# Summing a norm's squares on TensorE, feature tile by feature tile, in place of elementwise adds on POOL

## The chip, the cores and the metric

The kernel runs on one core of one Trainium2 chip. The metric is the device time of one execution in microseconds (us). The engines are named as the profile names them: PE is TensorE's matmul stream and PEld its weight loads, DVE is VectorE, ACT is ScalarE, POOL is GpSimd, SP is SyncE, whose queue issues the DMAs.

## What is computed

The reference is a two-layer encoder for 512 tokens of 1024 features in float32. Only its frame matters here:

```python
def rms_norm(x, g):
    y = xf * lax.rsqrt(jnp.mean(xf * xf, axis=-1, keepdims=True) + EPS)
    return (y * g.astype(jnp.float32)).astype(x.dtype)
...
    for l in range(DEPTH):
        h = rms_norm(x, attn_norm[l])
        proj = h @ w_in[l]
        ...                                  # four kinds of attention, 16 heads
        x = x + mix @ w_o[l]
        h = rms_norm(x, ffn_norm[l])
        x = x + (jax.nn.silu(h @ w_gate[l]) * (h @ w_up[l])) @ w_down[l]
    return rms_norm(x, final_norm)
```

So there are four norms ahead of dense products (attention and feed-forward, in two layers), and a final one. Each needs, for every token, the sum of the squares of its 1024 features.

## The kernel before

The activations lie transposed: x is eight tiles of 128 features by 512 tokens, x(0) to x(7). The norm isn't applied to the input of the products. `norm_inputs` makes from each x(k) the gained input, split in a high and a low part (`h[:, 0]` on ACT, or on DVE for odd k in the first norm; `h[:, 1]` by the scalar_tensor_tensor of line 209 on DVE), and the products run on these. The factor 1/rms of each token is multiplied into the results later. PE so doesn't need the sum of squares for its products, only whoever evacuates them does.

The sum of squares has two steps. `square` squares x(k) on ACT; the first square goes into the tile `ssq`, each later one into one of two buffers `sq`, which POOL adds to `ssq` (line 196), 128x512 elements at a time. After the eighth, `rms_column` lets PE sum over the 128 partitions: for each of four chunks of 128 tokens one product with the chunk of `ssq` as weights and one column of ones as the moving operand (line 225), into the first four columns of the PSUM bank "sm". DVE and POOL make the factor of it (`col`, `rcol`).

The four norms are called a0 (attention, layer 0), f0 (feed-forward, layer 0), a1 and f1 here. What surrounds each: a0 stands at the program's start, and its first consumer is the value projection `v_b` (line 382; weights `whi_vba`, `wlo_vba`, then `whi_vbb`, `wlo_vbb`, split from raw weights by ACT and DVE). f0 and f1 stand between the output projection (`wo`, whose results are added to x by DVE or, through a copy `po`, by POOL, line 609) and the gate and up products (`gu`, lines 178 to 183). a1 stands between the down products of layer 0 (`dn`) and `v_b` of layer 1.

Instructions are issued in order on each engine. What order that is, a scheduler decides when the program is built: it simulates the engines and places on each the instruction that it thinks ready first, in the program's order where several are. In attention a list of rates (`RATES`) mixes projections into the heads' work beforehand. The weights lie in four buffers `raw`, filled by DMAs from SP's queue.

Of the kernel before, what the change touches and what calls it, by code (L numbers as in the profile page):

```python
# [11 lines left out]
F32 = mybir.dt.float32  # L12
F32R = mybir.dt.float32r
AF = mybir.ActivationFunctionType
# [4 lines left out]
P = 128  # L19
D = 1024  # L20
S = 512
NL = 2
KD = D // P
# [41 lines left out]
def tile_encoder(ctx, tc, xT, gains, lamv, w_in, w_kr, w_d, w_o0, w_o1, w_o2, w_gu, w_dn,  # L65
                 t5, na_in, na_ed, onehot, crow, rope, na_mask, na_emask, out):
    nc = tc.nc
    pool = lambda name, **k: ctx.enter_context(tc.tile_pool(name=name, bufs=1, **k))

    cst = pool("cst")  # L70
# [9 lines left out]
    def stat_bank(nm):  # L80
        return ps.tile([P, 512], F32, tag="sm", name=nm, bufs=1)


    def wide(nm, dt=F32):

        return cst.tile([P, 2, S], dt, tag="h", name=nm, bufs=12)

    def res_tiles(nm):

        made = {}  # L90

        def at(k):
            if k // 2 not in made:
                made[k // 2] = wide(f"x{nm}{k // 2}")
            return made[k // 2][:, k % 2, :]

        return at, lambda k: at(k) is not None and made[k // 2]
# [8 lines left out]
    x, _ = res_tiles("in")  # L106
# [13 lines left out]
    ones = cst.tile([P, P], F32, name="ones")  # L120
# [69 lines left out]
    def square(acc, xk, k, nm):  # L190
        if k == 0:
            nc.scalar.activation(acc, xk, AF.Square)
            return
        sq = cst.tile([P, S], F32, tag="sq", name=f"sq_{nm}{k}", bufs=2)
        nc.scalar.activation(sq, xk, AF.Square)
        nc.gpsimd.tensor_tensor(acc, acc, sq, op=ALU.add)

    def norm_inputs(x, gcol, nm, lag, dve=()):

        hs = []  # L200
        acc = cst.tile([P, S], F32, tag="ssq", name=f"ssq_{nm}", bufs=1)
        for k in range(KD):
            h = wide(f"h_{nm}{k}", F32R)
            g = gn[:, gcol + k : gcol + k + 1]
            if k in dve:
                nc.vector.tensor_scalar(h[:, 0, :], x(k), g, None, op0=ALU.mult)
            else:
                nc.scalar.activation(h[:, 0, :], x(k), AF.Copy, scale=g)
            nc.vector.scalar_tensor_tensor(h[:, 1, :], x(k), g, h[:, 0, :].bitcast(F32),  # L209
                                           op0=ALU.mult, op1=ALU.subtract)  # L210
            hs.append(h)
            if k < lag:
                continue
            square(acc, x(k - lag), k - lag, nm)
        for k in range(KD - lag, KD):
            square(acc, x(k), k, nm)
        return hs, acc

    def rms_column(sums, n, nm, chunks=(0, 4), bank=None, mark=False):

        pt = bank or stat_bank(f"ms_{nm}")
        o = slice(0, chunks[1] - chunks[0])
        for c in range(*chunks):
            for i, t in enumerate(sums):
                mm = nc.tensor.matmul(pt[:, c - chunks[0] : c - chunks[0] + 1], t[:, c * P : (c + 1) * P], ones[:, :1],  # L225
                                 start=i == 0, stop=i == len(sums) - 1)
        col = cst.tile([P, 4], F32, tag="col", name=f"col_{nm}", bufs=4)
        nc.vector.tensor_scalar(col[:, o], pt[:, o], 1.0 / n, EPS, op0=ALU.mult, op1=ALU.add)
        r = cst.tile([P, 4], F32, tag="rcol", name=f"rcol_{nm}", bufs=4)
        nc.gpsimd.tensor_tensor(r[:, o], col[:, o], mhalf[:, o], op=ALU.pow)  # L230
        return (r, mm) if mark else r

    def spread_rows(r, nm, n, dst):

        pt = stat_bank(f"rows_{nm}")
        if n > 1:
            rep = cst.tile([P, S], F32, tag="sq", name=f"rep_{nm}", bufs=2)
            rep = rep.rearrange("p (c h d) -> p c h d", c=4, h=n)  # L240
            nc.vector.tensor_copy(rep, r.rearrange("p (h c) -> p c h", h=n).unsqueeze(3).to_broadcast([P, 4, n, P // n]))
        for c in range(4):
            col = r[:, c : c + 1].to_broadcast([P, P]) if n == 1 else rep[:, c].rearrange("p h d -> p (h d)")
            nc.tensor.transpose(pt[:, c * P : (c + 1) * P], col, ident)
        nc.scalar.copy(dst, pt)

    def rms_rows(r, nm):

        bc = cst.tile([P, S], F32, tag="bc", name=f"bc_{nm}", bufs=3)
        spread_rows(r, nm, 1, bc)  # L250
        return bc


    hs, ssq = norm_inputs(x, G_ATT, "a0", LAG0, HDVE)
# [50 lines left out]
    def attention(l, xsrc, x, hs, ssq, pl):  # L305
        k8 = lambda w, c: tuple(t.rearrange("p (k c) -> p k c", c=c) for t in w)
        ALL = slice(0, P)
        g = {}
# [62 lines left out]
        def v_tokens(lhs, rhs, nk, col, nm):  # L371

            v = g[f"v{nm}"] = v_tile(nm)
            pts = [acc_bank(f"v_{nm}{l}{i}") for i in range(2)]
            for k0 in range(0, nk, 4):
                for c in range(4):
                    o = pts[c // 2][:, (c % 2) * 256 : (c % 2) * 256 + 256]
                    t = slice(c * P, (c + 1) * P)
                    for k in range(k0, min(nk, k0 + 4)):
                        whi, wlo = rhs(k)  # L380
                        for i, (a, b) in enumerate(((0, whi), (1, whi), (0, wlo))):
                            nc.tensor.matmul(o, lhs[k][:, a, t], b, start=c % 2 == 0 and k == 0 and i == 0,
                                             stop=c % 2 == 1 and k == nk - 1 and i == 2, skip_group_check=True)
                            yield 0.5
                    if k0 + 4 >= nk and c % 2:
                        for i in (c - 1, c):
                            v_split(v, i, pts[i // 2][:, (i % 2) * 256 : (i % 2) * 256 + 256], col()[:, i : i + 1])

        def in_values(i, nm):
            wa = k8(slab(w_in[l, i], SLAB, nc.gpsimd, f"v{nm}a{l}"), 256)  # L390
            wb = k8(slab(w_in[l, i + 1], SLAB, nc.gpsimd, f"v{nm}b{l}"), 256)

            def col():
                if "rc" not in g:
                    g["rc"] = rms_column([ssq], D, f"at{l}")
                return g["rc"]

            yield from v_tokens(hs, lambda k: tuple(t[:, k % 4, :] for t in (wa if k < 4 else wb)), KD, col, nm)
# [512 lines left out]
        for part, ms in enumerate(PARTS):  # L911
            n = 4 // len(ms)
# [33 lines left out]
        for m, p, hh in HEADS:  # L946
            nm = "abcd"[m]
# [53 lines left out]
    def ffn(l, x, xpair, hs, ssq, pl):  # L1001
        turn = [0]

        def bank(nm):
            tag = ("acc", "sc", "tp")[turn[0] // 2 % 3]
            turn[0] += 1
            return ps.tile([P, 512], F32, tag=tag, name=nm, bufs=2)

        r_bc = rms_rows(rms_column([ssq], D, f"ff{l}"), f"ff{l}")
        act = []  # L1010
        for m in range(KF):
            pts = []
            for j in range(2):
                w = slab(w_gu[l, m, j], SLAB, nc.vector, f"gu{m}{j}{l}")
                w = tuple(t.rearrange("p (k c) -> p k c", c=P) for t in w)
                pt = bank(f"gu{m}{j}{l}")
                dense(pt, w, hs, slice(0, P))
                pts.append(pt)
            t = lambda n: pl.tile([P, S], F32, tag=n, name=f"{n}{m}_{l}", bufs=2)
            g, u, th = t("g"), t("u"), t("th")  # L1020
            nc.vector.tensor_tensor(g, pts[0], r_bc, op=ALU.mult)
            nc.scalar.activation(th, g, AF.Tanh, scale=0.5)
            nc.vector.scalar_tensor_tensor(u, pts[1], 0.5, r_bc, op0=ALU.mult, op1=ALU.mult)  # L1023
            nc.vector.scalar_tensor_tensor(th, th, 1.0, g, op0=ALU.add, op1=ALU.mult)
            nc.gpsimd.tensor_tensor(u, u, th, op=ALU.mult)  # L1025
            a = pl.tile([P, 2, S], F32R, tag="act", name=f"act{m}_{l}", bufs=KF)
            split(a[:, 0, :], a[:, 1, :], u)
            act.append(a)
        for m in range(KD - (l + 1 == NL)):
            pt = bank(f"dn{m}{l}")  # L1030
            for i, k0 in enumerate(range(0, KF, 8)):
                n = min(8, KF - k0)
                w = slab(w_dn[l, m][:, k0 * P : (k0 + n) * P], n * P, nc.vector, f"dn{m}{i}{l}")
                w = tuple(t.rearrange("p (k c) -> p k c", c=P) for t in w)
                dense(pt, w, act[k0 : k0 + n], slice(0, P), first=k0 == 0, last=k0 + n == KF)
            nc.vector.tensor_tensor(x(m), x(m), pt, op=ALU.add)
            if l + 1 < NL:
                nc.sync.dma_start(xd[:, m, :], x(m))
        if l + 1 == NL:
            last_tile(l, x, xpair, act, pl, bank)  # L1040
# [55 lines left out]
    for l in range(NL):  # L1096
        if l:
            hs, ssq = norm_inputs(x, G_ATT + KD * l, f"a{l}", 0)
        x, xpair = res_tiles(l)
        with tc.tile_pool(name=f"att{l}", bufs=1) as pl:  # L1100
            attention(l, xd if l else xT, x, hs, ssq, pl)
        hs, ssq = norm_inputs(x, G_FFN + KD * l, f"f{l}", 0)
# [127 lines left out]
```

## Time and profile before

| | us |
|---|---|
| median of 3 runs | 1343.3 (1340.87 to 1346.17) |
| profiled execution, its own time | 1343.78 |
| its span | 1342.0 |
| PE busy | 1290.7 (96% of the span), 6306 matmuls |
| PEld busy | 1066.8 (79%) |
| DVE busy | 773.3 (58%) |
| ACT busy | 561.3 (42%) |
| POOL busy | 469.8 (35%), 388 instructions |

The profiled execution's time is 1.8 us above its span and 0.5 us above the median. PE is busy almost all the time, the others about half of it or less; where PE stands still, the trace names the instruction that it waited for. An instruction's duration as listed includes time that overlaps with the next one; how much a stream of them takes is read from the distance between their starts.

### The profile page before, as it was taken

The page shows a single profiled execution, that of the slowest core. Times are in us where ns is not written, and L with a number is a line of the kernel's source. Part 1 is how long each engine was busy: PE and PEld are TensorE (multiplying, and loading weights), DVE is VectorE, ACT ScalarE, POOL GpSimd, SP SyncE. Part 2 cuts the span into 40 slices and gives each one's busy share as a digit, 9 for nine tenths or more (in the row PEclk, how much of TensorE's full clock was granted, in tenths as well). Part 3 has the DMA queues.
Part 4 walks back from the last instruction along what each step waited for, and adds up shares of the span by engine and source line. Part 5 has one row for each costly group of instructions (what it writes and reads, how often), then busy time and mean ns, then how long its engine had stood idle before and what let it go on. Part 6 is the DMA issues. An engine that isn't in the chain of part 4 may idle for free. (4 is left out here: it accounts for less than half of the span.)

```text
span 1342.0 us, 17137 instructions
## 1 busy us (share of the span) xinstructions
PE 1290.7 (96%) x6306; PEld 1066.8 (79%) x6306; DVE 773.3 (58%) x1309; ACT 561.3 (42%) x965; POOL 469.8 (35%) x388
## 2 busy tenths in 40 slices
PE   5998999999999999999999999999899999999997
PEld 5887878877888888888888777788688888888886
DVE  7499889866444444333236899887754444443232
ACT  3356656744333333232225666666533333332230
POOL 5257656535111111100135578454621111110100
PEclk9999999999999999999999899999999999999998
DMA  4552432112222222333345324322132222223321
GB/s 155 162 159 91 138 109 79 63 63 86 96 95 97 95 95 92 93 119 107 120 128 161 116 83 129 97 74 69 63 101 95 98 94 95 97 87 93 98 87 63
DMA packets 50484, 135.63 MB, mean 101 GB/s; under 512 B 7848, under 2 KB 12712, under 8 KB 50400
## 3 DMA queue, kind: packets, MB, share of 16 engines
q1 hardware_dynamic: 50400, 134.54, 32.2%
q8 instruction: 50, 0.82, 0.3%
q14 instruction: 34, 0.28, 0.1%
HBM read 119.01 MB, written 4.23 MB: 92 GB/s over the span
## 5 line engine op out<-in xcount | busy, mean ns | idle before, releaser
L180 PE MATMUL gu<-h_f,whi_gu 128*128 128x512 f32 x704 | 278.0, 395 | 1.3 <-DVE h_f L209 1.3
L178 PE MATMUL gu<-h_f,whi_gu 128*128 128x512 f32 x704 | 277.7, 395 | 0.1
L1025 POOL TENSOR_TENSOR u<-u,th 128x512 f32<-128x512 f32 x44 | 93.4, 2123 | 378.7 <-DVE u L1023 362.4
L183 PE MATMUL gu<-h_f,wlo_gu 128*128 128x512 f32 x704 | 177.9, 395 | 0.0
L180 PEld LDWEIGHTS gu<-h_f,whi_gu 128*128 128x128 f32 x704 | 132.5, 188 | 34.2 <-DVE h_f L209 3.9
L178 PEld LDWEIGHTS gu<-h_f,whi_gu 128*128 128x128 f32 x704 | 132.6, 188 | 31.7 <-DVE x L609 1.0
L183 PEld LDWEIGHTS gu<-h_f,wlo_gu 128*128 128x128 f32 x704 | 132.6, 188 | 30.9
L135 ACT CAST whi_gu<-raw_gu 128x1024 fp32r<-128x1024 f32 x88 | 92.5, 1052 | 112.5 <-PE gu L180 108.6
L178 PE MATMUL dn<-act,whi_dn 128*128 128x512 f32 x330 | 128.4, 389 | 0.0
L180 PE MATMUL dn<-act,whi_dn 128*128 128x512 f32 x330 | 128.4, 389 | 0.0
L165 DVE TENSOR_TENSOR wlo_gu<-raw_gu,whi_gu 128x1024 fp32r<-128x1024 f32 x88 | 110.8, 1259 | 20.0 <-ACT whi_gu L135 18.3
L632 ACT ACTIVATE e<-e,mx 128x512 f32<-128x512 f32 (+1 forms) x128 | 85.5, 669 | 66.7 <-DVE mx L630 61.5
L165 DVE TENSOR_TENSOR wlo_dn<-raw_dn,whi_dn 128x1024 fp32r<-128x1024 f32 (+1 forms) x45 | 51.0, 1134 | 100.4 <-PE dn L183 60.9
L1023 DVE SCALAR_TENSOR_TENSOR u<-gu,bc_ff 128x512 f32<-128x512 f32 x44 | 30.4, 691 | 128.5 <-PE gu L183 128.5
L135 ACT CAST whi_dn<-raw_dn 128x1024 fp32r<-128x1024 f32 (+1 forms) x45 | 44.2, 981 | 128.3 <-PE dn L180 111.3
L135 ACT CAST act<-u 128x512 fp32r<-128x512 f32 x44 | 27.3, 620 | 157.3 <-POOL u L1025 157.3
L183 PE MATMUL dn<-act,wlo_dn 128*128 128x512 f32 x330 | 82.1, 389 | 0.0
L140 DVE TENSOR_TENSOR tl<-tp,th 128x512 fp32r<-128x512 f32 x112 | 74.3, 681 | 7.8 <-ACT th L135 7.0
L630 DVE CUSTOM_DVE_ANT_0 e<-sc,t 128x512 f32<-128x512 f32 x96 | 65.0, 683 | 22.2 <-PE sc L697 19.5
L140 DVE TENSOR_TENSOR act<-u,act 128x512 fp32r<-128x512 f32 x44 | 32.7, 742 | 73.9 <-ACT act L135 73.6
L178 PEld LDWEIGHTS dn<-act,whi_dn 128*128 128x128 f32 x330 | 62.0, 188 | 12.9
L180 PEld LDWEIGHTS dn<-act,whi_dn 128*128 128x128 f32 x330 | 61.9, 188 | 12.9
(417 smaller groups left out, 2734.2 us busy)
## 6 DMA issues: line engine op xcount, KB each, us to landing
raw_gu<-in_w_gu_dram SPq DMA_DIRECT2D x88, 512.0 KB, 3.2
raw_dn<-in_w_dn_dram SPq DMA_DIRECT2D x32, 512.0 KB, 3.6
raw_wo<-in_w_o_dram SPq DMA_DIRECT2D x16, 512.0 KB, 4.0
t<-tb SPq DMA_DIRECT2D x16, 448.0 KB, 4.5
raw_dn<-in_w_dn_dram SPq DMA_DIRECT2D x16, 384.0 KB, 3.1
sb<-kbn SPq DMA_DIRECT2D x64, 64.0 KB, 2.0
sb<-qbn SPq DMA_DIRECT2D x64, 64.0 KB, 2.0
xin<-in_xT_dram SPq DMA_DIRECT2D x8, 256.0 KB, 5.9
```

The costliest lines, as they stand in the source:

```text
L135: nc.scalar.copy(out, src)
L140: engine(tag, usual).tensor_tensor(out, src, hi.bitcast(F32), op=ALU.subtract)
L165: lo_eng.tensor_tensor(lo[:, c], raw[:, c], hi[:, c].bitcast(F32), op=ALU.subtract)
L178: nc.tensor.matmul(pt, whi[:, k, wcol], xs[k][:, 0, :], start=first and k == 0, stop=False)
L180: nc.tensor.matmul(pt, whi[:, k, wcol], xs[k][:, 1, :], start=False, stop=False)
L183: nc.tensor.matmul(pt, wlo[:, k, wcol], xs[k][:, 0, :], start=False, stop=last and k == nk - 1)
L630: nc.vector.tensor_tensor_reduce(out=e, in0=sc, in1=bias, scale=1.0, scalar=BIG, op0=ALU.add, op1=ALU.min, accum_out=mx)
L632: nc.scalar.activation(e, src, AF.Exp, bias=mx, scale=-1.0, accum_out=den)
L1023: nc.vector.scalar_tensor_tensor(u, pts[1], 0.5, r_bc, op0=ALU.mult, op1=ALU.mult)
L1025: nc.gpsimd.tensor_tensor(u, u, th, op=ALU.mult)
```

## The change

For the four norms of `norm_inputs`, PE sums over the feature tiles too. Each square goes into a buffer `sq`, and four one-column products per tile (one per chunk of tokens) add it to the four columns of one PSUM bank, which the norm holds from its first product to its last. The tile `ssq`, POOL's adds and the four products at the end are gone there; what followed them is now `root_column`. The final norm keeps `square` and `rms_column`.

```diff
+    def square_sum(acc, xk, k, nm):
+        sq = cst.tile([P, S], F32, tag="sq", name=f"sq_{nm}{k}", bufs=2)
+        nc.scalar.activation(sq, xk, AF.Square)
+        for c in range(4):
+            nc.tensor.matmul(acc[:, c : c + 1], sq[:, c * P : (c + 1) * P], ones[:, :1], start=k == 0 and c == 0,
+                             stop=k == KD - 1, skip_group_check=True)
+
     def norm_inputs(x, gcol, nm, lag, dve=()):
         hs = []
-        acc = cst.tile([P, S], F32, tag="ssq", name=f"ssq_{nm}", bufs=1)
+        acc = stat_bank(f"ms_{nm}")
...
-            square(acc, x(k - lag), k - lag, nm)
+            square_sum(acc, x(k - lag), k - lag, nm)
...
-                    g["rc"] = rms_column([ssq], D, f"at{l}")
+                    g["rc"] = root_column(ssq, D, f"at{l}")
...
-        r_bc = rms_rows(rms_column([ssq], D, f"ff{l}"), f"ff{l}")
+        r_bc = rms_rows(root_column(ssq, D, f"ff{l}"), f"ff{l}")
```

Where the products stand in PE's queue is seen in the order of the built programs. In f0 before, PE had the four products of the sum (x4: four alike) between the second pair of gate and up weights and the third:

```order
L183 MATMUL gu010_3546<-h_f06_3478,wlo_gu010_3543 128x512
L183 MATMUL gu010_3546<-h_f07_3484,wlo_gu010_3543 128x512
L225 MATMUL ms_ff0_3493<-ones_93,ssq_f0_3443 128x1 x4
L178 MATMUL gu100_3588<-h_f00_3444,whi_gu100_3584 128x512
L180 MATMUL gu100_3588<-h_f00_3444,whi_gu100_3584 128x512
```

Now, on PE in f0, the products of the first squares stand among the last output projections (tiles 3 and 4 of `wo` are `wo230` and `wo240`):

```order
L183 MATMUL wo230_3412<-mix00_0_3312,wlo_wo200_3382 128x512
L183 MATMUL wo230_3412<-mix01_0_3374,wlo_wo200_3382 128x512
L204 MATMUL ms_f0_3464<-ones_93,sq_f00_3468 128x1 x4
L204 MATMUL ms_f0_3464<-ones_93,sq_f01_3477 128x1 x4
L178 MATMUL wo240_3429<-mix00_0_3312,whi_wo240_3424 128x512
L180 MATMUL wo240_3429<-mix00_0_3312,whi_wo240_3424 128x512
```

Squares 2, 3 and 4 follow behind `wo` tiles 5, 6 and 7, and squares 5, 6 and 7 among the first two `gu` tiles: eight fours in place of one, two of them side by side. f1 is alike.

In a1, on PE, all eight fours stand behind the last `dn` product; the first two are side by side, the other six among the products of `v_b`:

```order
L183 MATMUL dn70_5766<-act21_0_5154,wlo_dn720_5830 128x512
L204 MATMUL ms_a1_5854<-ones_93,sq_a10_5858 128x1 x4
L204 MATMUL ms_a1_5854<-ones_93,sq_a11_5867 128x1 x4
L396 MATMUL v_b10_5944<-whi_vba1_5932,h_a10_5855 128x256 x2
L396 MATMUL v_b10_5944<-wlo_vba1_5933,h_a10_5855 128x256
L396 MATMUL v_b10_5944<-whi_vba1_5932,h_a11_5864 128x256 x2
```

In a0 the first two fours stand ahead of PE's first product of `v_b`, the other six in three pairs among the 96 products of `v_b`: behind the 14th, the 40th and the 57th. On ACT in a0 before, the squares were mixed with the split of the second half of the weights (`whi_vbb`):

```order
L195 ACTIVATE sq_a05_137<-xin2_80 128x512
L135 CAST whi_vbb0_185<-raw_vbb0_183 128x512
L195 ACTIVATE sq_a06_140<-xin3_83 128x512
L135 CAST whi_vbb0_185<-raw_vbb0_183 128x512
L195 ACTIVATE sq_a07_143<-xin3_83 128x512
```

Now, on ACT in a0, four squares stand behind both halves of it:

```order
L218 ACTIVATE h_a06_118<-xin3_83,gn_69 128x512
L135 CAST whi_vbb0_211<-raw_vbb0_209 128x512 x2
L202 ACTIVATE sq_a04_148<-xin2_80 128x512
L202 ACTIVATE sq_a05_154<-xin2_80 128x512
L285 ACTIVATE lexp0_183<-lsum0_177 128x2
L285 ACTIVATE lexp1_193<-lsum1_187 128x2
L202 ACTIVATE sq_a06_160<-xin3_83 128x512
```

Away from the norms, the scheduler has also mixed the heads' scores and the projections differently in the first half of layer 0's attention; in layer 1's attention no instruction stands elsewhere.

## Rows read from the trace of the kernel before

**Rows 1.** Busy time by stretch: length, PE, PEld, DVE, ACT, POOL, granted clock, DMA:
```profile
0.00:31.00 31.00, 17.33 (x108) 16.22 (x109) 21.48 (x39) 12.29 (x21) 14.77 (x16) 0.94 0.52 167
306.00:331.00 25.00, 24.29 (x108) 18.83 (x107) 15.63 (x15) 10.93 (x15) 11.76 (x8) 1.00 0.25 85
667.00:686.00 19.00, 19.00 (x132) 17.71 (x131) 3.55 (x6) 3.83 (x5) 7.63 (x6) 1.00 0.54 163
961.00:986.00 25.00, 24.33 (x109) 19.02 (x109) 15.04 (x14) 10.36 (x14) 11.76 (x8) 1.00 0.25 85
130.00:140.00 10.00, 9.64 (x35) 7.88 (x36) 7.17 (x18) 5.49 (x12) 5.23 (x5) 0.70 0.18 52
```

**Rows 2.** PE's waits, whole run: us in total, times, longest:
```profile
PE v_b L382 <- DVE wlo_vbb L165: 3.3, 1, 3.3
PE v_b L382 <- DVE h_a L209: 2.9, 3, 1.4
PE gu L180 <- DVE h_f L209: 1.3, 4, 0.5
PE wo L178 <- DVE x L609: 1.0, 2, 0.7
```

**Rows 3.** PE in f0 in order of time: start, us, instruction:
```profile
319.05 0.95 PE L225 MATMUL ms_ff<-ones,ssq_f 128*128 128x1 f32 x8
319.86 0.47 PE L178 MATMUL gu<-h_f,whi_gu 128*128 128x512 f32 x1
320.17 0.39 PE L180 MATMUL gu<-h_f,whi_gu 128*128 128x512 f32 x1
320.40 0.39 PE L178 MATMUL gu<-h_f,whi_gu 128*128 128x512 f32 x1
```

**Rows 4.** DVE in a0 in order of time (wait in brackets):
```profile
6.80 0.48 DVE L206 TENSOR_SCALAR h_a<-xin,gn 128x512 fp32r<-128x512 f32 x1
7.32 2.30 DVE L209 SCALAR_TENSOR_TENSOR h_a<-xin,gn,h_a 128x512 fp32r<-128x512 f32 x2
10.15 1.50 DVE L206 TENSOR_SCALAR h_a<-xin,gn 128x512 fp32r<-128x512 f32 x1
20.27 1.40 DVE L209 SCALAR_TENSOR_TENSOR h_a<-xin,gn,h_a 128x512 fp32r<-128x512 f32 x2
```

**Rows 5.** POOL in a0 in order of time:
```profile
9.87 9.43 POOL L196 TENSOR_TENSOR ssq_a<-ssq_a,sq_a 128x512 f32<-128x512 f32 x6 [1.46 <-ACT sq_a L195]
```

**Rows 6.** PE in a0 in order of time:
```profile
9.68 0.58 PE L382 MATMUL v_b<-whi_vba,h_a 128*128 128x256 f32 x1 [1.39 <-DVE h_a L209]
...
22.64 0.40 PE L382 MATMUL v_b<-whi_vbb,h_a 128*128 128x256 f32 x2
...
23.00 0.40 PE L382 MATMUL v_b<-whi_vbb,h_a 128*128 128x256 f32 x2
...
23.94 0.63 PE L382 MATMUL v_b<-whi_vbb,h_a 128*128 128x256 f32 x2
...
24.58 0.63 PE L382 MATMUL v_b<-whi_vbb,h_a 128*128 128x256 f32 x2
...
26.50 0.55 PE L382 MATMUL v_b<-whi_vbb,h_a 128*128 128x256 f32 x2
...
30.17 0.39 PE L178 MATMUL sc_ip_kb<-h_a,whi_kb 128*128 128x512 f32 x1
```

**Rows 7.** ACT in order of time, in a0 and f0:
```profile
14.52 0.62 ACT L135 CAST whi_vbb<-raw_vbb 128x512 fp32r<-128x512 f32 x1 [1.07 <-DMA raw_vbb<-in_w_in_dram]
...
297.91 0.61 ACT L195 ACTIVATE sq_f<-x 128x512 f32<-128x512 f32 x1
```

**Rows 8.** PE in order of time: ends of both attentions, layer 1's start, one wait:
```profile
130.36 1.11 PE L772 MATMUL tp<-ident,e 128*128 128x128 f32 x4 [3.63 <-DVE e L702]
...
306.31 0.50 PE L178 MATMUL gu<-h_f,whi_gu 128*128 128x512 f32 x1
...
686.73 0.39 PE L178 MATMUL sc_ip_kb<-h_a,whi_kb 128*128 128x512 f32 x1
...
960.74 0.50 PE L178 MATMUL gu<-h_f,whi_gu 128*128 128x512 f32 x1
```

More of the change, by code (lines that the diff above doesn't have):

```diff
@@ L213, in norm_inputs @@
                 continue
-            square(acc, x(k - lag), k - lag, nm)
+            square_sum(acc, x(k - lag), k - lag, nm)
         for k in range(KD - lag, KD):
-            square(acc, x(k), k, nm)
+            square_sum(acc, x(k), k, nm)
         return hs, acc
@@ L226, in rms_column, with root_column @@
                                  start=i == 0, stop=i == len(sums) - 1)
+        r = root_column(pt, n, nm, o)
+        return (r, mm) if mark else r
+    def root_column(pt, n, nm, o=slice(0, 4)):
         col = cst.tile([P, 4], F32, tag="col", name=f"col_{nm}", bufs=4)
@@ L230, in rms_column @@
         nc.gpsimd.tensor_tensor(r[:, o], col[:, o], mhalf[:, o], op=ALU.pow)
-        return (r, mm) if mark else r
+        return r
     def spread_rows(r, nm, n, dst):
```

## The prediction

> **What bounds the kernel now.** I read the busy time by stretch first, around each of the four norms. In f0 and f1 PE is busy 24.3 of 25.0 us at the full granted clock, in a1 19.00 of 19.00 us; in a0, the first 31 us, only 17.3 [rows 1]. So at three of the four places whatever is added to PE's queue lengthens the run, unless it fills one of the short gaps, and at the fourth there are gaps. Whose they are, the waits of PE say: in a0 3.3 us for the low part of the weights `wlo_vbb` and 2.9 us for the low parts of h, in f0 and f1 together 1.3 us for the low part of h and 1.0 us for an addition to x [rows 2]. All of these come from DVE.
>
> Next I looked at what slows DVE there. In a0 the same tensor_scalar of 128x512 took 0.48 us at 6.80 and 1.50 us at 10.15, and two of the scalar_tensor_tensor took 2.30 us at 7.32 and 1.40 us at 20.27 [rows 4]. The long ones lie beside POOL's adds: six of these fill 9.87 to 19.30 without a gap [rows 5]. When POOL has finished, DVE is fast. The adds that the change removes are thus not free, though no chain of waits ends at their sum: they slow the engine that PE waits for.
>
> **What the change adds on PE.** The trace has the very operation: four one-column products of a 128x128 float32 weight tile. Each stands there as two matmul rows, and the four as x8. They start at 319.05, the next matmul at 319.86: 0.81 us, or 0.10 per row and 0.20 per product. The matmul behind them takes 0.31 to the one after it, where its neighbours take 0.23 [rows 3]. So a group of four costs 0.81 + 0.08 = 0.89 us, two groups side by side 2 x 0.81 + 0.08 = 1.70.
>
> The Trainium skill ("TensorE: Matmul & The Clock Gate", section "Back-to-back issue gap") lists a matmul of 1 to 64 columns at about 60 cycles, an issue floor of some 25 ns. By that the 112 added products, at two rows each, would cost an estimated 5.6 us, and the run would end near 1340. The row of 0.81 us for eight speaks against it here: something other than the column limits them, and the price of the row is measured in the same stream, so I take the row.
>
> f0, f1 and a1 each get eight groups, two of them side by side, in place of one: 1.70 + 6 x 0.89 - 0.89 = 6.15 us more. In a0 two groups stand ahead of `v_b`, where PE is idle anyhow: it waits until 9.68 but for two products [rows 6], and the first two squares need one early tile of x each. Were that cover gone, they would cost 1.70. The other three pairs cost 3 x 1.70 - 0.89 = 4.21. The bounds of the price: none, if the loads of the weights hid behind neighbouring matmuls (the group of rows 3 stands between 128x512 products and hid none), and, where the clock is low, 0.20 x 0.64 / 0.36 = 0.36 per product (that ratio from a0, below), which for a0's 24 products is 3.8 us more.
>
> **What it gives back.** In a0: the wait for `wlo_vbb`, 3.3; the waits for h behind the first one, 2.9 - 1.39 = 1.5; the start, since the two operations at 7.32 can take 1.40 in place of 2.30, 0.9; and the slow clock behind the long wait: from 23.94 to 26.50 three products take 0.64 us, where from 22.64 to 23.00 they take 0.36 [rows 6], 4 x 0.28 = 1.1. Together 6.8. For all of it to come, nothing else may be late. `whi_vbb` is released by its DMA at 14.52 [rows 7]; two halves of 0.6 on ACT and two of about 0.6 on DVE put the last `wlo_vbb` at 16.5. PE needs it behind 48 products and two pairs of groups: 8.8 + 14 x 0.21 + 34 x 0.12 + 3.4 = 19.2, so that wait is gone. Squares 4 and 5 stand behind `whi_vbb` on ACT and end at 14.52 + 4 x 0.6 = 16.9; PE comes to their products at 8.8 + 14 x 0.21 + 26 x 0.12 + 1.7 = 16.6 and waits 0.3, and all of `v_b` behind them waits with it. a0 is then worth -6.8 + 4.2 + 0.3 = -2.3. If DVE is slow for another reason, nothing comes back: +4.2.
>
> In f0 and f1: the 1.3 and 1.0 us of waits [rows 2], since POOL's additions to x (`po`) no longer queue behind adds of squares and DVE isn't slowed. Do the products wait for their squares there? Each comes behind an output tile or several `gu` products, 1 to 2 us apart, while ACT needs 0.61 for a square [rows 7], and a square waits only for the products of the one two before it. The worst case is x(7), which runs over PE, a copy on ACT, POOL's add, ACT's gain and the square, about 3.5 us behind the last output tile; its products stand 22 `gu` products and three groups later, 22 x 0.23 + 3 x 0.89 = 7.7 us. So I count no wait. Nor in a1: squares 2 to 7 now come late on ACT, only when PE has read the ones before them, but PE has 10 to 25 `v_b` products of 0.12 between pairs.
>
> What is removed from POOL, 28 adds, shortens nothing else: in a1 it worked in the shade of the `dn` products. The factor 1/rms comes earlier than before, and nobody waits for it.
>
> **Layer 0's attention** is mixed differently. I can't cost that row by row. There are two mixes of the same work in the trace: from the first `sc_ip_kb` to the first `gu` layer 0 takes 306.31 - 30.17 = 276.1 us [rows 6, 8] and layer 1 960.74 - 686.73 = 274.0 [rows 8]. They differ by 2.1; I take 0 and twice that difference, 4.2, to both sides.
>
> **Sum**: 3 x 6.15 - 2.3 (f0, f1) - 2.3 (a0) = +13.9 on the profiled 1343.8, 1357.7. That run lies 0.5 above the median, so 1357 is what I forecast for the median, 1.0% slower.
>
> **Rivals.**
> - *The passes hide behind their neighbours* (not slower). Then only edges remain: 24 groups or pairs less the 4 of before, 20 x 0.08 = 1.6, against 6.8 + 2.3 given back: 1336. For it speaks that PE loads weights ahead in dense streams; against it rows 3, measured in just such a stream. It decides only below 0.08 us per product, where 112 x 0.08 meets the 9.1 given back. Chance 0.04.
> - *The new mix of layer 0's attention removes its worst place.* A transpose waits 3.63 us for `e` at 130.36 [rows 8], and the granted clock is 0.70 in the ten microseconds there [rows 1], some 3.0 us lost: 13.9 - 6.6 = 7.3, 1350.5. All other waits of that mix would have to stay as they are. Chance 0.08.
> - *The relief doesn't come*, because DVE's long operations have another cause than POOL. Then 6.8 + 2.3 stay: 1366. Against it: with POOL's adds beside it the one tensor_scalar took three times as long. Chance 0.07.
> - *Products wait for squares.* PE's queue is in order; if at each of the 24 places ACT were half a square late, 24 x 0.3 = 7 us, 1364. With only two buffers `sq` ACT in turn waits for PE. From a whole square late at each place it is 1372. Chance 0.09.
>
> What is left, 0.72, is the forecast with its bounds: 1350 to 1362 from the attention's 4.2, half a microsecond of rounding at each norm, and parts of the relief missing or more. The rivals below and above leave some 0.1 on either side, so the range is 1350 to 1364. A difference of 0.5%, 6.7 us, is about what a measurement of this kernel can tell from none. Slower by more: the 0.72, the two slow rivals and a small part of the second, less a tail that meets the bound: 0.85. Within 0.5%: 0.11, most of it the attention's. Faster: 0.04, the first rival.
>
> **What would show it.** In the profile after, 0.81 us from the first to the end of a group, 0.10 per row; PE with 224 more matmul rows; the stretch from the first `gu` of f0 on shifted; a1 from the last `dn` to `sc_ip_kb` longer by 6.1 us with no wait named; in a0 DVE's scalar_tensor_tensor near 0.7 us each throughout, no wait for `wlo_vbb`, and `sc_ip_kb` starting near 28 in place of 30.17; layer 1's attention as long as before. The prediction is wrong if a group costs much less than 0.8 us, if waits for `sq` appear on PE, or if layer 0's attention moves by more than 4 us.

## The result

| | before | after |
|---|---|---|
| median, us | 1342.1 (1340.87 to 1346.17, 4 runs) | 1356.62 (1355.81 to 1357.4, 4 runs) |
| profiled execution, its own time | 1343.78 | 1355.97 |
| its span | 1342.0 | 1354.2 |

The changed kernel takes 1.0103 times as long, 95% interval 1.0078 to 1.0127: 14.5 us in the medians, 12.2 in the spans of the two profiled executions. The execution before that was profiled lies 1.7 us above its median, the one after 0.65 below.

The profile page of the changed kernel has this row of busy time (busy us, share, instructions):

```profile
PE 1314.4 (97%) x6530; PEld 1097.1 (81%) x6530; DVE 756.1 (56%) x1309; ACT 560.6 (41%) x965; POOL 424.2 (31%) x360
```

PE has the 224 added matmul rows (6306 before) and is busy 24 us longer; POOL is busy 46 us less and DVE 17 us less, and the run is longer all the same.

To see where 12.2 us went I cut the span of each kernel at eight places on PE that every kernel has: the end of `v_b` in a0, the `wo` product that waits some 1.7 us for DVE's `mix` near the end of an attention, the first `dn` product, the instruction behind the last `dn` product, the end of `v_b` in a1, and the same again in layer 1. For before these are 30.17, 291.36, 554.61, 674.35, 686.73, 946.08, 1209.02 and the span's end, 1342.0. Lengths in us, by differences of start times:

| kernel | a0 | att. 0 | f0, gu | dn 0 | a1 | att. 1 | f1, gu | rest | span |
|---|---|---|---|---|---|---|---|---|---|
| before | 30.17 | 261.19 | 263.25 | 119.74 | 12.38 | 259.35 | 262.94 | 132.98 | 1342.0 |
| after | 30.90 | 260.50 | 266.50 | 119.74 | 18.53 | 258.45 | 266.24 | 133.34 | 1354.2 |
| difference | +0.73 | -0.69 | +3.25 | 0 | +6.15 | -0.90 | +3.30 | +0.36 | +12.2 |
| predicted | -2.3 | 0 | +5.0 | 0 | +6.15 | 0 | +5.0 | 0 | +13.9 |

So the sum was right within 1.7 us, while the terms of a0, f0 and f1 were not; their errors have opposite signs.

**a1 and f0.** PE of the changed kernel in order of time, a1 first, then f0 (start, us, instruction).

```profile
677.64 1.84 PE L204 MATMUL ms_a<-ones,sq_a 128*128 128x1 f32 x16
679.34 0.48 PE L396 MATMUL v_b<-whi_vba,h_a 128*128 128x256 f32 x2
...
681.44 0.95 PE L204 MATMUL ms_a<-ones,sq_a 128*128 128x1 f32 x8
682.25 0.36 PE L396 MATMUL v_b<-wlo_vba,h_a 128*128 128x256 f32 x1
...
696.17 0.39 PE L178 MATMUL sc_ip_kb<-h_a,whi_kb 128*128 128x512 f32 x1
```

```profile
303.92 0.94 PE L204 MATMUL ms_f<-ones,sq_f 128*128 128x1 f32 x8
304.73 0.48 PE L178 MATMUL wo<-mix,whi_wo 128*128 128x512 f32 x1
```

In a1 a group takes 0.81 (681.44 to 682.25), as in [rows 3], the two side by side 1.70 (677.64 to 679.34), and nothing waits. The same 0.81 stands in f0, again without a wait in brackets. Of the waits of PE, whole run (us in total, times, longest), these two are of operands near a norm:

```profile
PE ms_a L204 <- ACT sq_a L202: 5.0, 1, 5.0
...
PE wo L178 <- DVE x L621: 0.4, 2, 0.3
```

The 5.0 for `sq_a` are the program's beginning. The list has no wait for `h_f`, for an operand of `v_b` or for a later square any more, and that of `wo` for x fell from 1.0 to 0.4 [rows 2].

**a0.** First DVE, then PE of the changed kernel, then busy time by stretch (length, PE, PEld, DVE, ACT, POOL, granted clock, DMA) for a0 and a1.

```profile
10.19 1.41 DVE L219 SCALAR_TENSOR_TENSOR h_a<-xin,gn,h_a 128x512 fp32r<-128x512 f32 x2
...
16.29 0.68 DVE L165 TENSOR_TENSOR wlo_vbb<-raw_vbb,whi_vbb 128x512 fp32r<-128x512 f32 x1
```

```profile
11.58 3.41 PE L204 MATMUL ms_a<-ones,sq_a 128*128 128x1 f32 x16
14.85 0.56 PE L396 MATMUL v_b<-whi_vba,h_a 128*128 128x256 f32 x1
...
15.42 0.63 PE L396 MATMUL v_b<-whi_vba,h_a 128*128 128x256 f32 x2
...
16.06 0.63 PE L396 MATMUL v_b<-whi_vba,h_a 128*128 128x256 f32 x2
...
20.54 1.88 PE L204 MATMUL ms_a<-ones,sq_a 128*128 128x1 f32 x16
22.29 0.37 PE L396 MATMUL v_b<-whi_vba,h_a 128*128 128x256 f32 x1
...
30.90 1.02 PE L303 MATMUL t<-oh,tab 32*8 32x512 f32 x2
```

```profile
0.00:31.00 31.00, 25.98 (x161) 25.83 (x162) 13.90 (x40) 12.30 (x21) 4.17 (x9) 1.00 0.54 167
677.60:696.20 18.60, 18.60 (x162) 18.56 (x161) 4.40 (x7) 5.24 (x9) 3.48 (x3) 1.00 0.48 148
```

DVE is as fast as was hoped: two scalar_tensor_tensor take 1.41 at 10.19, where [rows 4] had 2.30 for two, and the last `wlo_vbb` starts at 16.29. PE is busy 25.98 of 31 us, before 17.33 [rows 1], and yet `v_b` ends 0.73 us later. The reason is the distance of PE's rows. From 8.45 to 20.54 the products of `v_b` are 0.21 us apart (15.42 to 16.06 for three), and the pair at 11.58 takes 3.27; from 20.54 on a pair takes 1.75 and the products are 0.12 apart (three from 22.61 to 22.96). The ratio is that of PE's two clock levels, 1.2 and 2.4 GHz. The column of the granted clock says 1.00 for the whole stretch, so that here the spacing has to be read. Before, PE was at the wide spacing from 9.68 to 12.2 and once more, behind its long wait, up to 26.5 [rows 6].

### The profile page after: what moved, and what is told of

It reads as the page before. It is cut to its first block, busy times and chain, and to the rows that moved or that the text cites. A ratio compares the mean times of both kernels' runs of the same rounds, so it can differ in the third digit from the quotient of the medians.

```text
span 1354.2 us, 17562 instructions
## 1 busy us (share of the span) xinstructions
PE 1314.4 (97%) x6530; PEld 1097.1 (81%) x6530; DVE 756.1 (56%) x1309; ACT 560.6 (41%) x965; POOL 424.2 (31%) x360
## 5 line engine op out<-in xcount | busy, mean ns | idle before, releaser
L165 DVE TENSOR_TENSOR wlo_gu<-raw_gu,whi_gu 128x1024 fp32r<-128x1024 f32 x88 | 107.2, 1219 | 13.7 <-PE gu L183 10.5
L178 PEld LDWEIGHTS dn<-act,whi_dn 128*128 128x128 f32 x330 | 61.9, 188 | 13.0
L183 PEld LDWEIGHTS dn<-act,wlo_dn 128*128 128x128 f32 x330 | 62.0, 188 | 12.8
```

What stands on the lines that cost most here:

```text
L165: lo_eng.tensor_tensor(lo[:, c], raw[:, c], hi[:, c].bitcast(F32), op=ALU.subtract)
L178: nc.tensor.matmul(pt, whi[:, k, wcol], xs[k][:, 0, :], start=first and k == 0, stop=False)
L183: nc.tensor.matmul(pt, wlo[:, k, wcol], xs[k][:, 0, :], start=False, stop=last and k == nk - 1)
```

## Experiments

All ratios are to the kernel before, with the 95% interval; a time without a ratio is one run. Of each edit the lines that matter are shown. The parts of each kernel, cut as above:

| kernel | a0 | att. 0 | f0, gu | a1 | att. 1 | f1, gu | span |
|---|---|---|---|---|---|---|---|
| e1_no_adds | 23.10 | 260.40 | 262.78 | 12.30 | 258.09 | 261.70 | 1331.4 |
| e2_idle_adds | 28.42 | 262.02 | 266.25 | 18.53 | 259.55 | 266.50 | 1354.0 |
| e3_a0_late | 33.74 | 261.63 | 267.11 | 18.55 | 260.47 | 266.24 | 1360.3 |
| e4_f32r | 26.20 | 259.79 | 263.53 | 14.84 | 258.08 | 262.76 | 1337.6 |
| e5_late_squares | 22.23 | 270.78 | 263.45 | 12.38 | 257.90 | 262.77 | 1342.2 |
| e6_a1_block | 30.91 | 262.80 | 265.31 | 22.65 | 258.70 | 266.52 | 1360.0 |
| e7_ones_weights | 23.59 | 263.43 | 263.20 | 13.17 | 259.96 | 264.45 | 1340.2 |
| e8_cols32 | 27.00 | 260.49 | 266.21 | 18.56 | 260.90 | 266.22 | 1352.5 |
| e9_ones_a0 | 24.34 | 263.27 | 264.17 | 12.17 | 258.04 | 263.27 | 1337.6 |
| e10_f32r_a0 | 24.88 | 259.88 | 264.47 | 12.17 | 260.65 | 263.85 | 1338.4 |

One thing must be known to read the columns of f0 and f1: the long stream of `gu` products, which no edit touches, doesn't run at one pace everywhere. From each row of eight `wlo_gu` to the next are 24 products; here of e1_no_adds in f0:

```profile
326.01 2.03 PE L183 MATMUL gu<-h_f,wlo_gu 128*128 128x512 f32 x8
331.62 2.03 PE L183 MATMUL gu<-h_f,wlo_gu 128*128 128x512 f32 x8
```

Such a round takes 5.60 us on average in e3_a0_late, e4_f32r, e7_ones_weights, e9_ones_a0, e10_f32r_a0 and in f0 of e1_no_adds, and 5.577 in all others, f1 of e1_no_adds included, at a granted clock of 1.00 in both. Over the 44 rounds of such a part it makes 1.0 us. No trace here shows what decides it.

My theory ahead of the experiments: products cost 0.10 us a row wherever PE is the bound, and POOL's adds, by slowing DVE, were what made PE wait in a0, f0 and f1. The rival: POOL has no part in the waits; the products fill time that PE would have waited anyhow.

### The adds alone, taken away and put back

e1_no_adds, before with

```diff
-        nc.gpsimd.tensor_tensor(acc, acc, sq, op=ALU.add)
+        if nm == "fin":
+            nc.gpsimd.tensor_tensor(acc, acc, sq, op=ALU.add)
```

> The kernel before, with POOL's 28 adds of squares left out in the four norms (the sum then holds the first square alone); nothing is added on PE. If POOL's adds are what makes DVE late, PE loses its waits in a0 and its six late starts in f0 and in f1 (3.1 us each by the distance of the starts): v_b of a0 ends some 4 to 7 us earlier than at 30.17, f0 and f1 are 3 us shorter each, a1 as before; 1342 - 12 = about 1330. Rival 1, the products of the change filled the gaps and POOL's adds had no part in them: f0 and f1 as before, 1342 to 1336. Rival 2, DVE's long operations in a0 have another cause: a0 as before too, 1342.

Measured: 1333.44, ratio 0.9933 (0.9914 to 0.9953). PE in a0 (the next instruction behind `v_b`), and in f0:

```profile
23.10 1.02 PE L290 MATMUL t<-oh,tab 32*8 32x512 f32 x2
```

```profile
297.89 0.63 PE L183 MATMUL wo<-mix,wlo_wo 128*128 128x512 f32 x2
298.63 0.51 PE L178 MATMUL gu<-h_f,whi_gu 128*128 128x512 f32 x1
...
301.52 0.40 PE L178 MATMUL gu<-h_f,whi_gu 128*128 128x512 f32 x1
301.91 0.49 PE L180 MATMUL gu<-h_f,whi_gu 128*128 128x512 f32 x1
303.06 0.50 PE L178 MATMUL gu<-h_f,whi_gu 128*128 128x512 f32 x1 [0.65 <-ACT po L602]
```

a0 is relieved in full. `v_b` ends at 23.10, and one product `t` of 0.95 us, which comes behind it in the kernel before, lies inside: 30.17 - 23.10 + 0.95 = 8.0 us. 0.9 of it are the four products, which come ahead of `v_b` here; the other 7.1 are the relief that I put at 6.8. In f0 the gain is 0.47, in f1 1.24; without the slower `gu` rounds f0's would be 1.5. PE still starts late three times: 298.63 (0.74 behind two rows that need 0.46), 301.91 (0.39 in place of 0.23) and 303.06 (1.15 in place of 0.23), now for ACT's copy `po`. With the 0.10 that the instruction behind each late one loses where it stands at 0.33, that is 1.6 us, where the kernel before has 3.1 of the kind (below). So without POOL's adds about half of the lateness in f0 is gone. Some of that may be due to the four products of the sum and the four of `rows_ff`: they come earlier here, among the last `wo` tiles, and fill time as the products of the change do. The forecast of 3 us in each of f0 and f1 was more than twice what came.

e2_idle_adds, the changed kernel with

```diff
+        if k:
+            junk = cst.tile([P, S], F32, tag="ssq", name=f"jq_{nm}{k}", bufs=1)
+            nc.gpsimd.tensor_tensor(junk, sq, sq, op=ALU.add)
```

> The changed kernel, with POOL's 28 additions put back beside the products (each square is added to itself, into a tile that nobody reads). PE's order is that of the changed kernel. If POOL's adds slow DVE, DVE's scalar_tensor_tensor in a0 takes 1.1 to 1.8 us again; in f0 and f1 the late starts come back as far as the products haven't given DVE the time: 0 to 3 us each. My theory, that the relief comes from POOL, says 1357 to 1363. Rival, the products alone took the waits away by delaying PE: 1356.6 within 1.

Measured: 1357.29, ratio 1.0118 (1.0092 to 1.0145), the time of the changed kernel. f0 and f1 have not moved (266.25 and 266.50 against 266.50 and 266.24), though POOL adds there as before. For f0 and f1 the rival was right: PE has no late start there with POOL's adds or without, so the eight groups of products are enough to take the waits away. In a0 it was neither. DVE is slow again, but `v_b` ends earlier than in the changed kernel, with the same order on PE. DVE first, then PE:

```profile
10.29 2.19 DVE L222 SCALAR_TENSOR_TENSOR h_a<-xin,gn,h_a 128x512 fp32r<-128x512 f32 x2
```

```profile
11.79 1.84 PE L207 MATMUL ms_a<-ones,sq_a 128*128 128x1 f32 x16
13.49 0.36 PE L399 MATMUL v_b<-whi_vba,h_a 128*128 128x256 f32 x1
...
21.81 1.95 PE L207 MATMUL ms_a<-ones,sq_a 128*128 128x1 f32 x16 [1.19 <-ACT sq_a L202]
...
28.42 1.02 PE L306 MATMUL t<-oh,tab 32*8 32x512 f32 x2
```

The pair at 11.79 takes 1.70 here, at 11.58 in the changed kernel 3.27: PE came to the higher clock level just ahead of this pair, there only behind the next 26 `v_b` products. The kernel with 32 columns, below, has nearly the same order too and comes to the higher level at the same place: its a0 is 27.00, 3.9 us less than 30.90. In e2_idle_adds 2.5 of that are left, since PE waits there for slow DVE, and 1.19 us for a square (21.81).

### Where a0's products stand

e3_a0_late, the changed kernel with a0's products in `rms_column`, behind `v_b`'s 72nd product:

```diff
-                    g["rc"] = root_column(ssq, D, f"at{l}")
+                    sums = [t[:, j, :] for t in sqs for j in range(2)]
+                    g["rc"] = root_column(ssq, D, f"at{l}") if l else rms_column(sums, D, f"at{l}", after=mms[-1])
```

> The changed kernel, with a0's 32 products moved together behind PE's 72nd product of v_b, where before the four stood; the eight squares stay in eight buffers. f0, a1 and f1 as in the changed kernel. Theory: the early products in a0 are what keeps PE's spacing at 0.21 us per v_b product until 20.5; without them the spacing falls to 0.12 some 4 us after PE's start, v_b ends near 28.5 in place of 30.9, and the run is some 2.4 us shorter, 1354. Rival: PE's spacing stays at 0.21 until about 20 whatever stands there: v_b ends near 31.5, 1357. The mix of layer 0's attention is another one than in the changed kernel and may add up to 4 us to either side, so v_b's end and the spacing tell these apart.

Measured: 1363.69, ratio 1.0160 (1.0139 to 1.0181). PE in a0, then busy time by stretch:

```profile
12.52 0.41 PE L399 MATMUL v_b<-whi_vba,h_a 128*128 128x256 f32 x2
...
19.48 10.84 PE L238 MATMUL ms_at<-ones,sqa 128*128 128x1 f32 x64
30.18 0.56 PE L399 MATMUL v_b<-wlo_vbb,h_a 128*128 128x256 f32 x1
30.54 0.63 PE L399 MATMUL v_b<-whi_vbb,h_a 128*128 128x256 f32 x2
```

```profile
16.00:20.00 4.00, 4.00 (x37) 4.00 (x35) 3.60 (x9) 0.20 (x1) 2.50 (x2) 1.00 0.47 135
20.00:25.00 5.00, 5.00 (x36) 5.00 (x37) 0.62 (x4) 0.20 (x1) 0.07 (x1) 0.76 0.33 105
25.00:31.00 6.00, 6.00 (x29) 6.00 (x30) 0.16 (x1) 0.00 (x0) 0.40 (x1) 0.50 0.00 0
```

Both forecasts missed, 1354 and 1357. The spacing of `v_b` is 0.12 from 12.4 on, as the theory had it for `v_b` without products ahead of it. That alone doesn't show that the early products hold the spacing wide, since e2_idle_adds has them and is at 0.12 from 11.6 on. The traces of all kernels give this:

| kernels | narrow spacing in a0 from, us |
|---|---|
| no product with a square as weights between the first `v_b` products: e7_ones_weights, e3_a0_late, e9_ones_a0, e1_no_adds, before, e5_late_squares | 11.9, 12.3, 12.8, 12.9, 13.4 (PE stands still before), 13.7 |
| with them: e2_idle_adds, e8_cols32, e10_f32r_a0, e4_f32r, e6_a1_block, after | 11.6, 11.8, 12.4, 16.5, 20.4, 20.5 |

Such products can go with a late rise, then, and needn't. The time of the row was wrong outright. 64 rows should take 6.5 us; they took 10.7, and behind them `v_b` goes on at 0.21. The granted clock, 1.00 up to 20, is 0.76 from 20 to 25 and 0.50 from 25 to 31, that is the level of 1.2 GHz, while PE's row shows no gap. `v_b` ends at 33.74, 2.8 us later than in the changed kernel; the rest of the 6.1 us by which the span is longer lies in the attentions and f0.

e6_a1_block puts the same row into a1, some 690 us after the program's beginning. Edit:

```diff
-                    g["rc"] = root_column(ssq, D, f"at{l}")
+                    sums = [t[:, j, :] for t in sqs for j in range(2)]
+                    g["rc"] = rms_column(sums, D, f"at{l}", after=mms[-1]) if l else root_column(ssq, D, f"at{l}")
```

> The changed kernel, with a1's 32 products together behind the 72nd product of v_b, in place of eight groups; everything else as in it. If a long row of one-column products lets the granted clock fall, as the row of 64 in a0 suggests (10.7 us, clock 0.50 behind it), these 64 rows take 9 to 11 us in place of 6.5, the products behind them 0.21 each, and a1 is 4 to 6 us longer than in the changed kernel, 23 to 25 from the last dn product to the end of v_b. Rival, it was the program's beginning that did it: 6.5 us for the row, clock 1.00, a1 18.5 as in the changed kernel.

Measured: 1361.75 in one run; a1 22.65, 4.1 us longer than in the changed kernel (forecast 4 to 6). PE, then busy time by stretch:

```profile
688.60 9.82 PE L238 MATMUL ms_at<-ones,sqa 128*128 128x1 f32 x64
698.28 0.56 PE L399 MATMUL v_b<-whi_vbb,h_a 128*128 128x256 f32 x1
```

```profile
688.00:692.00 4.00, 4.00 (x39) 4.00 (x37) 0.00 (x0) 0.00 (x0) 0.03 (x1) 1.00 0.39 131
692.00:696.00 4.00, 4.00 (x25) 4.00 (x24) 0.00 (x0) 0.00 (x0) 0.00 (x0) 0.60 0.01 4
696.00:700.00 4.00, 4.00 (x20) 4.00 (x20) 0.16 (x1) 0.25 (x1) 1.02 (x1) 0.50 0.00 0
```

The row takes 9.68, the granted clock falls from 1.00 to 0.60 and 0.50 while PE is busy 4.00 of 4.00 us. So it isn't the program's beginning: a long row of one-column products takes PE to the lower level. Groups of eight or sixteen rows between wider products, as in f0 and a1 of the changed kernel, leave the granted clock at 1.00.

### What the price consists of

e4_f32r, the changed kernel with

```diff
-        sq = cst.tile([P, S], F32, tag="sq", name=f"sq_{nm}{k}", bufs=2)
+        sq = cst.tile([P, S], F32R, tag="sq", name=f"sq_{nm}{k}", bufs=2)
...
-            nc.tensor.matmul(acc[:, c : c + 1], sq[:, c * P : (c + 1) * P], ones[:, :1], start=k == 0 and c == 0,
+            nc.tensor.matmul(acc[:, 2 * c : 2 * c + 2], sq[:, c * P : (c + 1) * P], ones_r[:, :2], start=k == 0 and c == 0,
```

> The changed kernel, with the squares and the column of ones in float32r, and two columns of ones (each token's sum comes out twice): one matmul row per product in place of two. If the price goes by the row, a group takes 0.40 us in place of 0.81: f0, a1 and f1 are 3.2 us shorter each and a0 3 to 5: 1356.6 - 13.5 = 1343. Rival, the price goes by the instruction or by the bytes of the weights: a group stays at 0.8, 1356.6.

Measured: 1341.68, ratio 0.9991 (0.9980 to 1.0002). PE in a1:

```profile
672.61 0.50 PE L206 MATMUL ms_a<-ones_r,sq_a 128*128 128x2 f32 x4
672.97 0.36 PE L398 MATMUL v_b<-whi_vba,h_a 128*128 128x256 f32 x1
```

Four rows, 0.36 us: 0.09 per row, and half the rows. f0 is 2.97 us shorter than in the changed kernel, a1 3.69, f1 3.48, a0 4.70, part of the last by an earlier rise of the clock level (16.5 in place of 20.5, table above). The price goes by the row, as the forecast of 1343 had it.

e8_cols32 asks which side of a row costs: 32 moving columns in place of one.

```diff
-            nc.tensor.matmul(acc[:, c : c + 1], sq[:, c * P : (c + 1) * P], ones[:, :1], start=k == 0 and c == 0,
+            nc.tensor.matmul(acc[:, 32 * c : 32 * c + 32], sq[:, c * P : (c + 1) * P], ones[:, :32], start=k == 0 and c == 0,
```

> The changed kernel with 32 columns of ones in place of one as the moving operand (the same sums 32 times). If the price is that of the weights, a group stays at 0.81 us and 0.10 per row, 1356.6 within the attention's variation of 2. Rival, the moving columns count: a group is 1.0 us or longer, f0, a1 and f1 1.5 us longer each or more, above 1361.

Measured: 1354.24 in one run. PE in f0:

```profile
307.05 0.97 PE L204 MATMUL ms_f<-ones,sq_f 128*128 128x32 f32 x8
307.86 0.48 PE L178 MATMUL gu<-h_f,whi_gu 128*128 128x512 f32 x1
```

A group stays at 0.81, f0, a1 and f1 are the changed kernel's within 0.3 us; the run is 2.4 us shorter, with a0 3.9 shorter (27.00) and attention 1 2.4 longer. At 32 columns a row costs what it costs at one.

e7_ones_weights exchanges the sides:

```diff
-        for c in range(4):
-            nc.tensor.matmul(acc[:, c : c + 1], sq[:, c * P : (c + 1) * P], ones[:, :1], start=k == 0 and c == 0,
-                             stop=k == KD - 1, skip_group_check=True)
+        nc.tensor.matmul(acc[:2], ones_r, sq, start=k == 0, stop=k == KD - 1)
...
+        row = cst.tile([P, S], F32, tag="sq", name=f"row_{nm}", bufs=2)[:1]
+        nc.vector.tensor_copy(row, acc[:1, :])
+        pt = stat_bank(f"col_{nm}")
+        for c in range(4):
+            nc.tensor.matmul(pt[:, c : c + 1], row[:, c * P : (c + 1) * P], ones[:1, :1], start=True, stop=True)
```

> The changed kernel with the operands swapped in all four norms: two columns of ones are the weights and the square (float32r, 128x512) is the moving operand, one matmul per feature tile in place of four products; DVE copies the row of sums out of PSUM, and four products of one partition turn it into columns. If the price is that of loading the squares as weights, a tile costs 0.23 to 0.33 us in place of 0.81 to 0.89, a1 takes 14 to 15 us (before 12.38, changed 18.53), f0 and f1 are no longer than before, a0 ends v_b near 24.5: 1342 - 6 + 2 = 1338. Rival, each switch to other weights and back costs as much as a group of one-row products: as with float32r squares, 1341.7.

Measured: 1341.45, ratio 0.9983 (0.9974 to 0.9992). PE in a1:

```profile
673.20 0.39 PE L205 MATMUL ms_a<-sq_a,ones_r 128*2 128x512 f32 x1
673.43 0.40 PE L404 MATMUL v_b<-whi_vba,h_a 128*128 128x256 f32 x2
...
685.28 1.05 PE L245 MATMUL col_at<-ones,row_at 1*128 1x1 f32 x8
```

A feature tile costs 0.23 us, in place of 0.81. a1 is only 0.8 longer than before, while the four products that make columns of the row have moved behind it, to 685.28. The squares are now read as 512 moving columns, and only two columns are loaded as weights. The forecast of 1338 was missed all the same: attention 0 is 2.2 us longer than before, and f1 1.5, 1.0 of it by the slower `gu` rounds. With the two runs above this shows that what one pays for in the change is matmul rows that each load a 128x128 square as weights, two per product in float32, and not the moving columns. No run has a row with few columns on both sides, so a price of some 0.1 us for any row isn't told apart from that of the load.

The Trainium skill ("TensorE: Matmul & The Clock Gate", section "LDWEIGHTS (loading the stationary operand)") gives the time of a weight load by the number of its columns; for 128 its formula gives an estimated 107 ns. The traces are near it: 0.09 to 0.10 us per row, one load each.

### Relief without a price

e5_late_squares, the kernel before with a0's squares issued behind the split of `vbb`:

```diff
+            if l == 0 and i == IN_B:
+                with tc.issue_after(casts[-1].ins):
+                    for k in range(KD):
+                        square(ssq[1], ssq[0](k), k, "a0")
```

> The kernel before, with one thing moved: a0's eight squares stand on ACT behind both halves of the split of the second weights (whi_vbb), so that POOL's adds come when DVE's work for v_b is done; nothing is added on PE, the other norms are as before. If POOL's adds beside DVE's long operations are what costs a0, DVE's scalar_tensor_tensor takes 0.7 us each throughout, v_b ends near 22 (the kernel without adds: 23.1, with 0.95 of another table's product and 0.81 of the four products before it) in place of 30.17, and the run is some 7 us shorter, 1335. Rival: the sum now comes some 8 us later in the program, the factor 1/rms with it, and what waits for it gives the gain back: 1339 to 1343.

Measured: 1345.23, ratio 1.0014 (1.0005 to 1.0023). PE:

```profile
22.23 0.39 PE L180 MATMUL sc_ip_kb<-h_a,whi_kb 128*128 128x512 f32 x1
...
33.52 1.05 PE L229 MATMUL ms_at<-ones,ssq_a 128*128 128x1 f32 x8
```

a0 is 7.9 us shorter, and attention 0 gives back 9.6: POOL's last three adds, at 1.67 us each, end at 33.5, PE waits 3.3 us in three places from 36.7 to 51.3 for what hangs on the sum or stands behind it, and the mix of the attention behind it is another one, with a wait of 3.2 at 157.5. a0 was relieved as forecast, and the rival was right on the run, which lies even above its 1339 to 1343. How much of the 9.6 is the late sum, and how much the other mix, this run doesn't tell.

e9_ones_a0 and e10_f32r_a0 change a0 alone, the one as in e7_ones_weights, the other as in e4_f32r; in `norm_inputs`

```diff
+OLD = ('f0', 'a1', 'f1')
...
+        old = nm in OLD
+        add = square if old else square_sum
```

> The kernel before with a0 alone changed, in the way of the kernel with ones as weights; f0, a1 and f1 are summed by POOL as before. Layer 0's attention is mixed as in the kernel before. By the parts measured so far: a0 ends v_b at 23.6 in place of 30.17, all else as before: 1342.5 - 6.6 = 1336, with 1.5 us of variation from both attentions. Rival: the attention behind it gives it back, as it did for the late squares: 1341 to 1343.

> The kernel before with a0 alone changed, by one-row products of float32r squares; f0, a1 and f1 are summed by POOL as before. Layer 0's attention is mixed as in the kernel with float32r squares everywhere. By the parts measured so far: a0 26.2 in place of 30.17, attention 0 259.8 in place of 261.2, the rest as before: 1342.5 - 5.4 = 1337. Rival: as for the one above, 1341 to 1343.

Measured: e9_ones_a0 1341.24, ratio 0.9985 (0.9976 to 0.9995); e10_f32r_a0 1339.84, ratio 0.9972 (0.9962 to 0.9983). PE of the second, in a0:

```profile
24.88 1.02 PE L308 MATMUL t<-oh,tab 32*8 32x512 f32 x2
```

a0 gains 5.8 and 5.3 us, the spans are 4.4 and 3.6 shorter, and the medians miss the forecasts of 1336 and 1337: the first lies where its rival had it, the second between. In e9_ones_a0 attention 0 is 2.1 longer though its mix is that of the kernel before but for its first 34 us, in e10_f32r_a0 f0 and attention 1 are 1.2 and 1.3 longer with the same instructions as before; 1.0 of f0's 1.2 are the slower `gu` rounds. Parts that no edit touches vary that much from kernel to kernel (attention 1 from 257.90 to 260.90). Of a0's relief 0.15% and 0.28% are left in the medians; e10_f32r_a0 is the fastest kernel here whose sum is complete, and beats both the kernel before and the changed one.

## Why the prediction was right, point by point

**The total.** 1357 was forecast and 1356.6 measured, in part by luck. Between the profiled executions a0 came out 3.0 us dearer than forecast, f0 and f1 together 3.45 cheaper, and the two attentions and the rest, put at nothing, 1.2 shorter. What was right by its mechanism is the price of a group on PE, and the relief in a0.

**The price on PE.** Right where PE is at the higher level: 0.81 a group, a1 +6.15, no wait for a square. That it fits to the hundredth is chance: a pair takes 1.70 up to the next product, and the 0.08 that this one loses comes on top (679.34 to 679.66, for two that else take 0.24), so it costs 1.78 where the prediction had 1.70 with the 0.08 inside. The price is that of rows that load weights, not of columns (e4_f32r, e8_cols32, e7_ones_weights). By the rule that the prediction weighs, of the Trainium skill ("TensorE: Matmul & The Clock Gate", section "Back-to-back issue gap"), it would have been a quarter of it, 25 ns per row; the trace, with 0.10 us per row, does not agree with that.

**a0 -2.3: wrong, it was +0.73.** The relief was there: 7.1 by e1_no_adds for 6.8, and DVE, `wlo_vbb` and the squares came as I said. The step that failed is the price of the products in a0, "the other three pairs cost 3 x 1.70 - 0.89 = 4.21". The three pairs are 5.1 us of that; against e1_no_adds, where `v_b` without `t` ends at 22.15, they cost 30.90 - 22.15 = 8.75. The difference is the lower level: the pair at 11.58 takes 1.57 more than at the higher, and 40 products of `v_b` are spaced at 0.214 in place of 0.119, where in e1_no_adds 21 are, which is 19 x 0.095 = 1.8; with 3 x 1.78 for the pairs the sum is 8.7. I had this end among the bounds ("0.36 per product", 3.8 us more) and took the other. What I didn't see is that PE can stay at the lower level while these products fill its row, here until 20.5, and that a long row of them takes it there from the higher level (e3_a0_late, e6_a1_block). How much comes of it varies with one and the same order: e2_idle_adds was at the higher level from 11.6 on. With a rise as early as there, a0 would have been some 3.9 us shorter (27.00 in e8_cols32) and the term near -3.2: -2.3 was within reach of nearly the same order.

**f0 and f1 +5.0 each: +3.25 and +3.30.** The step "the 1.3 and 1.0 us of waits" was mis-sized, and its reason half wrong. I took what comes back from the listed waits. A listed wait is only the idle time beyond the modelled end of the instruction ahead. PE of the kernel before in f0, the first of six late starts:

```profile
301.57 0.63 PE L183 MATMUL wo<-mix,wlo_wo 128*128 128x512 f32 x2
302.93 0.50 PE L178 MATMUL wo<-mix,whi_wo 128*128 128x512 f32 x1 [0.72 <-DVE x L609]
303.27 0.39 PE L180 MATMUL wo<-mix,whi_wo 128*128 128x512 f32 x1
```

The two `wlo_wo` rows need 0.46, so the next should start at 302.03. It starts 0.90 later, 0.72 of which is in brackets, and the one behind it follows after 0.34 in place of 0.23: 1.01 us in all. Read so, the starts at 302.93, 304.61, 306.31, 309.13, 313.06 and 314.76 are late by 3.1 us, where the brackets have 0.72, 0.17 and 0.49, 1.38. In the changed kernel none of the six is left, and 6.15 - 3.1 is what f0 cost. And they went not because POOL stopped adding (without the adds about half of the lateness stays, e1_no_adds; with adds and products none of it, e2_idle_adds) but because the products took up the time in which PE would have stood.

**Layer 0's attention: -0.69.** The wait of 3.63 [rows 8] went, others came, as in the rival that I gave 0.08; on balance nothing, within the variation of this part.

**Rivals.** The passes did not hide. The relief did come. Products did not wait for squares in the changed kernel.

What stays open: what decides when PE comes to the higher level in a0, with one order of instructions at 11.5 us or at 20.5. Moving only the two early groups, with the others in place, wasn't tried, and no kernel's a0 was profiled twice. Open too is what decides the pace of the `gu` rounds.

## What to carry to other kernels

A product with one column isn't cheap when it has weights of its own: here each of its matmul rows cost 0.09 to 0.10 us, with one column or 32. Before one moves a sum to TensorE, put the wide operand on the moving side, or make each product one row. When a stall's worth is to be estimated, read it from the distance of starts, as one reads a price; what the list of waits shows was less than half of it here. And filling gaps is worth the gaps' length only: half the price of the products was covered by gaps in f0, and nothing of it in a1, where PE had none.

## What was not expected of the hardware

- A row of 64 one-column matmuls without a gap takes PE from 2.4 to 1.2 GHz: granted clock 1.00, then 0.60 and 0.50, 9.7 and 10.7 us in place of 6.5, and what follows at half speed for some us (e6_a1_block, e3_a0_late).
- At a program's start products are spaced for 1.2 GHz (0.214 for 256 columns) while the column of the granted clock says 1.00.
- POOL's adds of 128x512 beside DVE's work slow DVE only where they meet it: 2.19 for two scalar_tensor_tensor at 10.29 in e2_idle_adds, 1.41 in the changed kernel, without adds.
- A stream of 128x512 products with the same instructions and a granted clock of 1.00 runs at one of two paces, 5.577 or 5.600 us for 24 products, from kernel to kernel and in e1_no_adds from layer to layer.
